# A two-layer hybrid decoder trunk on one core: projection blocks as one 512-column and one 256-column matmul, with an addition at eviction, and shorter softmaxes

## The chip, the cores and the metric

The kernel runs on one core of a Trainium2 chip. The metric is the device time of one execution in microseconds (us), the median of several runs. TensorE is PE in the rows (PEld is its weight loads), VectorE is DVE, ScalarE is ACT, GpSimd is POOL, and SyncE (SP) issues the weight transfers.

## What is computed

Two layers work on 256 tokens of width 2048, in fp32. Each layer normalises x, projects it with one large input matrix, feeds three mixers (sparse attention, an S5 state space, pooling), gates each, concatenates, projects with w_out, normalises and adds to x. Cut to what the change touches:

```python
def masked_softmax(s, mask, axis):
    s = jnp.where(mask, s.astype(jnp.float32), NEG_INF)
    m = jnp.max(s, axis=axis, keepdims=True)
    e = jnp.where(mask, jnp.exp(s - m), 0.0)
    return e / jnp.maximum(jnp.sum(e, axis=axis, keepdims=True), 1e-30)
...
p_c = masked_softmax(s_c, mask_c, -1)
...
p = masked_softmax(sc, mask, (-2, -1))
...
p_w = masked_softmax(s_w, mask_w, -1)
...
o = gates[..., 0, :] * o_c + gates[..., 1, :] * o_s + gates[..., 2, :] * o_w
```

With 256 tokens every causal block is among the selected ones, so the selected and the window branch are both plain causal attention, over different keys and values.

## The kernel before

**Two-part numbers.** Each fp32 operand of a large product is split into a high and a low part of a format that TensorE multiplies in one pass; the product is high times high, high times low and low times high, summed in PSUM. ACT makes the high part of each weight half piece (L311, 128x1024), DVE the low part (L317, the difference). The activations stand transposed in two tiles, hT[0] (high) and hT[1] (low), 16 blocks of 128 rows by 256 tokens.

**Pieces.** The weights of a layer come as a stream of pieces in the order of use, in halves of 512 KB. They land in a ring of five buffers (raw, RAWB = 5), and are split into a ring of four high (whi) and four low (wlo) buffers. Most pieces are 128 output columns of the input matrix: u5 (4 pieces), kc, vc, ks, kw (2 each), q, za (8 each), z5, up, zp (4 each), 40 in a layer and 80 in all. Function do_b handles such a piece: it splits the next piece's halves (split(n + 1, h)), multiplies the present one (mm_b, 16 blocks), and evicts it with what the piece asks for. For each block mm_b calls mm3, three matmuls of 256 columns into one PSUM tile pp, of which there are three:

```python
T.matmul(out, lhsT=lh, rhs=rh, start=start, stop=False, **kw)
T.matmul(out, lhsT=lh, rhs=rl, start=False, stop=False, **kw)
T.matmul(out, lhsT=ll, rhs=rh, start=False, stop=stop, **kw)
```

They are lines 387, 388 and 389. Other pieces are ck and cv (weights of the key and value compression, used straight from the raw buffer, L1111), vs and vw (values, with the activations as the stationary side), gl (the S5 mixer's GLU) and wo (output projection, 512 columns at a time, also through mm3).

**Evictions.** u5: two ACT copies (L1044, L1045). kc and vc: two DVE additions (cmp_blocks, L642). ks and kw: rope, four DVE operations, then a split (L697 to L700). q: an ACT copy to qf (L1128) and rope. za, z5, zp: silu2, a Tanh on ACT (L881) and one DVE operation (L882). up: an ACT copy (L1181).

**Chains.** Attention, the S5 scan, compression and pooling are generators that advance a step at a time between half pieces (slot), by a credit of estimated TensorE time. Outside the start and the layer boundary the tile scheduler then orders each engine's queue. att_unit handles one head, one tile of queries and two branches: scores, mask added to the diagonal (L724), maximum (L725), times -scale (L726), two Exp with sums, floor at 1e-30 (L732), reciprocal, gate, two scalings, transposes. There are 32 of them. att_cmp is the same for the compressed branch, 8 in all.

Of the kernel before, what the change touches and what calls it, by code (L numbers as in the profile page):

```python
# [18 lines left out]
NKT = D // 128  # L19
# [10 lines left out]
# column offsets of the input projection  # L30
# [4 lines left out]
def piece_plan():  # L35
    """Weight pieces of one layer in the order of use: (kind, index, cols per half)."""
    b = [("vs", 0), ("vs", 1)] + [("u5", t) for t in range(4)]
    early = [("kc", 0), ("kc", 1), ("vc", 0), ("vc", 1), ("ks", 0), ("ks", 1), ("kw", 0), ("kw", 1),
             ("vw", 0), ("vw", 1), ("vw", 2)]
    cmp_ = [("ck", i) for i in range(4)] + [("cv", i) for i in range(4)]  # L40
    mid = []
    for i, e in enumerate(early):
        mid.append(e)
        if i >= 2:
            mid += cmp_[:2]
            del cmp_[:2]
# [30 lines left out]
# columns of the per-layer small parameters  # L77
# [7 lines left out]
# columns of the per-layer S5 matrices, pool and compression matrices  # L85
# [5 lines left out]
for _n, _w in (("ident", 128), ("mask", 128), ("cos", 256), ("sin", 256), ("cmask", 32), ("valid", 2),  # L91
               ("rowm", 2), ("i2", 32), ("ptab", 64), ("tm", 16), ("m01", 64), ("hpi", 1)):
    CN[_n] = (_o, _o + _w)
    _o += _w
# [3 lines left out]
def constants():  # L98
# [7 lines left out]
    put("mask", np.where(i[None, :] <= i[:, None], 0.0, -1e30).astype(np.float32))  # L106
# [31 lines left out]
def body(ctx, tc, a):  # L138
# [113 lines left out]
        # cos and sin of 4 theta b and 32 theta a, a and b in 0 .. 7  # L252
# [38 lines left out]
    def split(n, h, hold=False):  # L291
        if n >= len(stream):
            return
        l, k, i, off = stream[n]
        if k in ("ck", "cv"):
            return
        hc = halves(k, i)
        w = hc[h]
        raw = raws.pop((n, h))
        if k == "wo" and i in (12, 13):  # L300
            if i == 12 and h == 0:
                X["hTw"] = tuple(z.rearrange("p k s -> p (k s)") for z in new_hT())
# [37 lines left out]
    def grab(*tags):  # L340
        """wait until every one of the tags has a free buffer, then hold them"""
# [5 lines left out]
    def demand(*tags):  # L347
        """the same for the stream of pieces: run the chains until the buffers are free"""
# [26 lines left out]
    def split_f32r(hi, lo, src, scale=None, hi_eng=None):  # L375
        """hi + lo == src * scale, both float32r"""
# [7 lines left out]
    def mm3(out, l, r, start, stop, **kw):  # L384
        """three passes: hi*hi, hi*lo, lo*hi"""
# [6 lines left out]
    def rstd_of(parts_, first=None):  # L392
        """(sum of the four parts / D + EPS) ** -0.5; first: what rstd_first made of three of them"""
# [11 lines left out]
    def norm_scale(x, r, gpre, hbuf, c):  # L405
        """hbuf = x * r * gpre in quarter c of x and hbuf [128, D]"""
# [3 lines left out]
    def norm_high(t, hbuf, hT, c):  # L410
        """high part of quarter c of hbuf transposed; returns what makes the low part"""
# [12 lines left out]
    def vsel(n, t, c):  # L424
        """values of the selected branch, tile t, from quarter c of hT"""
# [5 lines left out]
    def norm_vsel(n, t, x, r, gpre, hbuf, hT, lag):  # L431
        """the norm of tile t and its values, quarter after quarter"""
# [12 lines left out]
    def new_hT():  # L445
        return tuple(big.tile([128, NKT, S], F32R, name=nm("hT"), tag=f"hT{i}", bufs=1) for i in range(2))

# [1 line left out]
    def s5_chain(l):  # L449
# [22 lines left out]
        def tables(hf):  # L472
            """cos and sin of 4 theta j, j = 8 a + b, for the state tiles 8 hf .. 8 hf + 7"""
# [29 lines left out]
        def spread(dst, x, y, op, k0):  # L503
            """x op y, group by group into the block diagonal of dst"""
# [43 lines left out]
        for t in range(4):  # L548
# [5 lines left out]
            # transposed input matrices and the lag kernels  # L554
# [81 lines left out]
    def cmp_blocks(which, g, p, l):  # L636
# [3 lines left out]
        pv = p[:, :256].rearrange("p (n j) -> p j n", j=16)  # L640
# [53 lines left out]
    def rope(p, dst_hi, dst_lo):  # L694
        r1 = st([128, 256], "r1", bufs=2)
        r2 = st([128, 256], "r2", bufs=2)
        V.tensor_tensor(r1, p[:, :256], C["cos"], op=ALU.mult)  # L697
        V.tensor_tensor(r2[0:64], p[64:128, :256], C["sin"][64:128], op=ALU.mult)
        V.tensor_tensor(r2[64:128], p[0:64, :256], C["sin"][0:64], op=ALU.mult)
# [4 lines left out]
    def att_unit(pr, j, t):  # L704
        """one head of the pair, one tile of queries: scores .. transposed weights"""
# [15 lines left out]
        sv = st([128, 5, 2], "sv", bufs=4)  # L721
        P = st([128, 2, nk], "P", bufs=2)
        diag = pv[:, :, nk - 128:nk]
        V.tensor_tensor(diag, diag, bc(C["mask"][:, None, :], [128, 2, 128]), op=ALU.add)  # L724
        V.tensor_reduce(sv[:, 0], pv, axis=AX.X, op=ALU.max)  # L725
        V.tensor_scalar(sv[:, 1], sv[:, 0], -SCALE, None, op0=ALU.mult)  # L726
        for b in range(2):
            A.activation(P[:, b], pv[:, b], AF.Exp, scale=SCALE, bias=sv[:, 1, b:b + 1],  # L728
                         accum_out=sv[:, 2, b:b + 1])
        give("sc")  # L730
        yield 0.1 + 0.001 * 2 * nk
        V.tensor_scalar(sv[:, 3], sv[:, 2], 1e-30, None, op0=ALU.max)  # L732
        V.reciprocal(sv[:, 3], sv[:, 3])
        V.tensor_mul(sv[:, 4], X["gates"][:, t, 3 * h + 1:3 * h + 3], sv[:, 3])
        for b in range(2):
            A.activation(P[:, b], P[:, b], AF.Copy, scale=sv[:, 4, b:b + 1])  # L736
# [17 lines left out]
    def att_cmp(pr):  # L754
# [22 lines left out]
        sv = st([128, 4, 2, 2], "scv", bufs=2)  # L777
# [7 lines left out]
        V.tensor_scalar(sv[:, 1], sv[:, 1], 1e-30, None, op0=ALU.max)  # L785
        gt = X["gates"][:, :, 6 * p0:6 * p0 + 6].rearrange("p t (j b) -> p t j b", j=2)[:, :, :, 0]
        V.reciprocal(sv[:, 1], sv[:, 1])
        V.tensor_tensor(sv[:, 2], gt, sv[:, 1], op=ALU.mult)
        V.tensor_tensor(sv[:, 3], sv[:, 2], bc(C["valid"][:, :, None], [128, 2, 2]), op=ALU.mult)
        V.tensor_tensor(sc, sc, bc(sv[:, 3, :, :, None], [128, 2, 2, 16]), op=ALU.mult)  # L790
# [88 lines left out]
    def silu2(dst, p):  # L879
        """dst = 2*silu(p)"""  # L880
        A.activation(dst, p, AF.Tanh, scale=0.5)  # L881
        V.scalar_tensor_tensor(dst, dst, 1.0, p, op0=ALU.add, op1=ALU.mult)  # L882

# [48 lines left out]
    # start  # L932
# [91 lines left out]
    while n < nst:  # L1024
# [5 lines left out]
        if kind == "u5":  # L1030
# [23 lines left out]
        elif kind in ("kc", "vc"):  # L1054
# [8 lines left out]
            def ev(p, i=i, w=w, l=l):  # L1063
                cmp_blocks(w, i, p, l)

            do_b(n, ev)
        elif kind in ("ks", "kw"):
# [3 lines left out]
            do_b(n, lambda p, i=i, b=b: rope(p, X["kr"][:, 0, i, b, :], X["kr"][:, 1, i, b, :]))  # L1071
# [8 lines left out]
        elif kind == "vw":  # L1080
# [5 lines left out]
            for h in range(2):  # L1086
# [4 lines left out]
                if k0 == 16:  # L1091
                    vr = X["vr"]
                    for t in range(2):
# [3 lines left out]
                        V.tensor_scalar(X["gates"][:, t], X["gates"][:, t], 0.5, 0.5, op0=ALU.mult, op1=ALU.add)  # L1097
                slot(nk * 6 * w / 2400 - 1.1 * hv[h] / 1024 + 0.6)
# [17 lines left out]
        elif kind in ("q", "za"):  # L1116
# [9 lines left out]
            def ev(p, j=j, pr=pr, kind=kind):  # L1126
                if kind == "q":
                    A.activation(pr["qf"][:, j, :], p[:, :256], AF.Copy)  # L1128
                    rope(p, pr["qr"][:, 0, j], pr["qr"][:, 1, j])
# [8 lines left out]
                else:  # L1138
                    silu2(pr["zt"][:, j, :], p[:, :256])
# [4 lines left out]
        elif kind == "z5":  # L1144
            if i == 0:
                X["z5"] = a8([128, 4, 256])
            do_b(n, lambda p, i=i: silu2(X["z5"][:, i, :], p[:, :256]))
# [28 lines left out]
        elif kind == "up":  # L1176
            def ev(p, i=i, l=l):
# [3 lines left out]
                A.activation(pu[:, 16:], p[:, :256], AF.Copy)  # L1181
# [3 lines left out]
        elif kind == "zp":  # L1185
            def ev(p, i=i):
                demand("zs")
                z = st([128, 2, 256], "zs", bufs=2)[:, 0]
                silu2(z, p[:, :256])
                X["zp", i] = z  # L1190
            do_b(n, ev)
        else:
# [32 lines left out]
            def update(t, r, sq=None):  # L1225
                """x += og * r, with the sums of squares or the store"""
# [162 lines left out]
```

## Time and profile before

| what | value |
|---|---|
| time, median of 3 runs | 893.35 us (893.23 to 893.95) |
| profiled execution | span 890.6 us from the first to the last instruction; the page has no other time of it |
| median less span | 2.7 us, outside the recorded instructions |
| PE busy | 857.6 us, 96% of the span |
| DVE busy | 645.3 us, 72% |
| ACT busy | 481.3 us, 54% |
| granted TensorE clock | mean 0.988; below full at the start, at the layer boundary and at the very end |
| memory | 159.37 MB read and 4.19 MB written, 184 GB/s over the span |

A matmul's busy time runs from its start to a modelled end and overlaps the next matmul's. What a matmul costs in a stream is therefore the distance from its start to the next one's start (below: its pitch), not the duration in its row. An engine's busy share is an average over stages: the start, two layers of about 415 us each and the boundary between them near 450 us.

### The profile page before, as it was taken

The page shows a single profiled execution, that of the slowest core. Times are in us where ns is not written, and L with a number is a line of the kernel's source. Part 1 is how long each engine was busy: PE and PEld are TensorE (multiplying, and loading weights), DVE is VectorE, ACT ScalarE, POOL GpSimd, SP SyncE. Part 2 cuts the span into 40 slices and gives each one's busy share as a digit, 9 for nine tenths or more (in the row PEclk, how much of TensorE's full clock was granted, in tenths as well). Part 3 has the DMA queues.
Part 4 walks back from the last instruction along what each step waited for, and adds up shares of the span by engine and source line. Part 5 has one row for each costly group of instructions (what it writes and reads, how often), then busy time and mean ns, then how long its engine had stood idle before and what let it go on. Part 6 is the DMA issues. An engine that isn't in the chain of part 4 may idle for free. (4 is left out here: it accounts for less than half of the span.)

```text
span 890.6 us, 17313 instructions
## 1 busy us (share of the span) xinstructions
PE 857.6 (96%) x6848; PEld 795.3 (89%) x6848; DVE 645.3 (72%) x1264; ACT 481.3 (54%) x933; POOL 51.8 (6%) x71
## 2 busy tenths in 40 slices
PE   4899999999999999999979999999999999999996
PEld 3898889999999999888869988999999999998884
DVE  6886779796987866556478556978968878665563
ACT  5454635676566754445445525475847767344440
POOL 3302000000000000000040300000000000000000
PEclk9899999999999999999989999999999999999998
DMA  7565766524344665456445558663534347455642
GB/s 288 179 188 185 268 235 225 172 104 162 121 165 143 227 241 194 172 201 224 182 165 199 183 197 312 211 213 99 173 123 155 140 144 295 154 177 189 197 146 95
DMA packets 46042, 165.75 MB, mean 186 GB/s; under 512 B 5508, under 2 KB 5764, under 8 KB 44808
## 3 DMA queue, kind: packets, MB, share of 16 engines
q1 hardware_dynamic: 43352, 154.15, 50.3%
q0 software_dynamic: 2608, 10.49, 3.3%
q8 instruction: 54, 0.88, 0.4%
q14 instruction: 28, 0.23, 0.1%
HBM read 159.37 MB, written 4.19 MB: 184 GB/s over the span
## 5 line engine op out<-in xcount | busy, mean ns | idle before, releaser
L311 ACT ACTIVATE whi<-raw 128x1024 fp32r<-128x1024 f32 (+2 forms) x238 | 248.4, 1046 | 256.3 <-PE pp L388 82.8
L317 DVE TENSOR_TENSOR wlo<-raw,whi 128x1024 fp32r<-128x1024 f32 (+1 forms) x236 | 284.4, 1207 | 123.7 <-ACT whi L311 123.1
L389 PE MATMUL pp<-hT,wlo 128*128 128x256 f32 x1280 | 365.7, 286 | 0.5 <-DVE wlo L317 0.5
L387 PE MATMUL pp<-hT,whi 128*128 128x256 f32 x1280 | 364.8, 285 | 0.8 <-ACT whi L311 0.8
L388 PE MATMUL pp<-hT,whi 128*128 128x256 f32 x1280 | 363.5, 284 | 0.0
L387 PEld LDWEIGHTS pp<-hT,whi 128*128 128x128 f32 x1280 | 245.0, 191 | 6.1 <-issue 3.8
L389 PEld LDWEIGHTS pp<-hT,wlo 128*128 128x128 f32 x1280 | 245.0, 191 | 2.4 <-DVE wlo L317 0.7
L388 PEld LDWEIGHTS pp<-hT,whi 128*128 128x128 f32 x1280 | 245.0, 191 | 1.7 <-issue 1.0
L387 PE MATMUL acc<-whi,m 128*128 128x512 f32 x112 | 44.4, 397 | 0.0
L389 PE MATMUL acc<-whi,m 128*128 128x512 f32 x112 | 44.4, 397 | 0.0
L388 PE MATMUL acc<-wlo,m 128*128 128x512 f32 x112 | 44.1, 394 | 0.0
L388 PE MATMUL pp<-wlo,m 128*128 128x512 f32 x112 | 43.6, 389 | 0.0
L389 PE MATMUL pp<-whi,m 128*128 128x512 f32 x112 | 43.6, 389 | 0.0
L387 PE MATMUL pp<-whi,m 128*128 128x512 f32 x112 | 43.6, 389 | 0.0
L507 ACT ACTIVATE m<-m 64x256 f32<-64x256 f32 x64 | 26.4, 413 | 5.9 <-DVE m L505 4.9
L728 ACT ACTIVATE P<-sc,sv 128x128 f32<-128x128 f32 (+1 forms) x64 | 26.2, 418 | 5.4 <-DVE sv L726 3.7
L925 POOL DMA_DIRECT2D a<-in_gpost x2 | 1.1, 557 | 451.4 <-PE tr L743 451.4
L378 ACT ACTIVATE a<-tr 128x256 fp32r<-128x256 f32 (+1 forms) x32 | 15.6, 488 | 18.6 <-PE tr L743 18.5
L387 PEld LDWEIGHTS acc<-whi,m 128*128 128x128 f32 x112 | 21.5, 192 | 4.5
L388 PEld LDWEIGHTS acc<-wlo,m 128*128 128x128 f32 x112 | 21.5, 192 | 4.5
L389 PEld LDWEIGHTS acc<-whi,m 128*128 128x128 f32 x112 | 21.4, 191 | 4.5
L736 ACT ACTIVATE P<-P,sv 128x128 f32<-128x128 f32 (+1 forms) x64 | 25.4, 448 | 0.0
(295 smaller groups left out, 1384.4 us busy)
## 6 DMA issues: line engine op xcount, KB each, us to landing
raw<-in_w SPq DMA_DIRECT2D x272, 512.0 KB, 3.6
raw<-in_w SPq DMA_DIRECT2D x8, 420.0 KB, 4.2
a<-in_x SPq DMA_DIRECT2D x4, 512.0 KB, 6.9
a<-in_gpost POOLq DMA_DIRECT2D x2, 1024.0 KB, 4.8
a<-in_x POOLq DMA_DIRECT2D x2, 1024.0 KB, 6.3
xs<-a SPq DMA_DIRECT2D x2, 1024.0 KB, 4.1
a<-xs POOLq DMA_DIRECT2D x2, 1024.0 KB, 7.4
out_dram<-a SPq DMA_DIRECT2D x8, 256.0 KB, 2.4
```

The costliest lines, as they stand in the source:

```text
L311: A.activation(hi[:, :w], raw[:, :w], AF.Copy)
L317: V.tensor_tensor(lo[:, :w], raw[:, :w], hi[:, :w].bitcast(F32), op=ALU.subtract)
L378: A.activation(hi, src, AF.Copy)
L387: T.matmul(out, lhsT=lh, rhs=rh, start=start, stop=False, **kw)
L388: T.matmul(out, lhsT=lh, rhs=rl, start=False, stop=False, **kw)
L389: T.matmul(out, lhsT=ll, rhs=rh, start=False, stop=stop, **kw)
L507: A.activation(dst[64 * g:64 * g + 64, :, k0:k0 + 4, 16 * g:16 * g + 16], x[64 * g:64 * g + 64], AF.Copy)
L728: A.activation(P[:, b], pv[:, b], AF.Exp, scale=SCALE, bias=sv[:, 1, b:b + 1], accum_out=sv[:, 2, b:b + 1])
L736: A.activation(P[:, b], P[:, b], AF.Copy, scale=sv[:, 4, b:b + 1])
L925: nc.gpsimd.dma_start(g, bass.AP(tensor=src.tensor, offset=src.offset, ap=[[0, 128], [1, D]]))
```

## The change

The two activation tiles become one tile, so that the high and the low half of a block can be read as one operand of 512 columns. mm2 takes the place of mm3 in mm_b: the high weights times both halves in one matmul over all 512 columns of pp, then the low weights times the high half into the first 256. join adds the two halves of pp: an ACT copy of columns 256 to 511 into a small buffer (r2, of which there are two), then a DVE addition. Every one of the 80 pieces is evicted through join, and rope, cmp_blocks and silu2 then read its sum from SBUF. In att_unit two tensor_tensor_reduce, one for each branch, add the mask (now 256 columns wide), scale by the negative scale and take the minimum; the floor is gone. In att_cmp the floor and the multiplication by the valid mask are gone, and the gates are multiplied by it once a layer (gcmp). RAWB is 5 in both kernels.

```diff
-for _n, _w in (("ident", 128), ("mask", 128), ("cos", 256), ("sin", 256), ("cmask", 32), ("valid", 2),
+for _n, _w in (("ident", 128), ("mask", 256), ("cos", 256), ("sin", 256), ("cmask", 32), ("valid", 2),
...
+    def mm2(p, l, r, start, stop):
+
+        T.matmul(p.rearrange("p (z s) -> p z s", z=2), lhsT=l[0], rhs=r, start=start, stop=False)
+        T.matmul(p[:, :256], lhsT=l[1], rhs=r[:, 0], start=False, stop=stop)
+
+    def join(p, y):
+
+        z = st([128, 256], "r2", bufs=2)
+        A.activation(z, p[:, 256:], AF.Copy)
+        V.tensor_tensor(y, p[:, :256], z, op=ALU.add)
+        return y
...
     def new_hT():
-        return tuple(big.tile([128, NKT, S], F32R, name=nm("hT"), tag=f"hT{i}", bufs=1) for i in range(2))
+        z = big.tile([128, 2, NKT, S], F32R, name=nm("hT"), tag="hT", bufs=1)
+        return z[:, 0], z[:, 1], z
...
-        diag = pv[:, :, nk - 128:nk]
-        V.tensor_tensor(diag, diag, bc(C["mask"][:, None, :], [128, 2, 128]), op=ALU.add)
-        V.tensor_reduce(sv[:, 0], pv, axis=AX.X, op=ALU.max)
-        V.tensor_scalar(sv[:, 1], sv[:, 0], -SCALE, None, op0=ALU.mult)
+
         for b in range(2):
-            A.activation(P[:, b], pv[:, b], AF.Exp, scale=SCALE, bias=sv[:, 1, b:b + 1],
-                         accum_out=sv[:, 2, b:b + 1])
+            V.tensor_tensor_reduce(out=pv[:, b], in0=pv[:, b], in1=C["mask"][:, 256 - nk:], scale=-SCALE,
+                                   scalar=3.0e38, op0=ALU.add, op1=ALU.min, accum_out=sv[:, 0, b:b + 1])
+        for b in range(2):
+            A.activation(P[:, b], pv[:, b], AF.Exp, scale=-1.0, bias=sv[:, 0, b:b + 1],
+                         accum_out=sv[:, 1, b:b + 1])
         give("sc")
         yield 0.1 + 0.001 * 2 * nk
-        V.tensor_scalar(sv[:, 3], sv[:, 2], 1e-30, None, op0=ALU.max)
...
     def silu2(dst, p):
...
-        A.activation(dst, p, AF.Tanh, scale=0.5)
-        V.scalar_tensor_tensor(dst, dst, 1.0, p, op0=ALU.add, op1=ALU.mult)
...
+        join(p, dst)
+        t = st([128, 256], "r1", bufs=2)
+        A.activation(t, dst, AF.Tanh, scale=0.5)
+        V.scalar_tensor_tensor(dst, t, 1.0, dst, op0=ALU.add, op1=ALU.mult)
...
-            mm3(p[:, :256], (hi[:, sl], lo[:, sl]), (hT[0][:, k, :], hT[1][:, k, :]), k == 0, k == 15)
+            mm2(p, (hi[:, sl], lo[:, sl]), hT[2][:, :, k, :], k == 0, k == 15)
...
             def ev(p, i=i):
-                A.activation(X["uT"][:, i, :], p[:, :256], AF.Copy)
-                A.activation(X["utb"][:, i], p[:, :256].rearrange("p (j b) -> p b j", b=4), AF.Copy)
+                u = join(p, X["uT"][:, i, :])
+                A.activation(X["utb"][:, i], u.rearrange("p (j b) -> p b j", b=4), AF.Copy)
...
-                cmp_blocks(w, i, p, l)
+                cmp_blocks(w, i, join(p, st([128, 256], "qf")), l)
...
-                    A.activation(pr["qf"][:, j, :], p[:, :256], AF.Copy)
-                    rope(p, pr["qr"][:, 0, j], pr["qr"][:, 1, j])
+                    rope(join(p, pr["qf"][:, j, :]), pr["qr"][:, 0, j], pr["qr"][:, 1, j])
```

**PE, first layer, where the first vc piece ends and the ck pieces begin.** Of a block the last matmuls are shown (pp is the piece's PSUM tile, whi and wlo the split weights, acc<-raw the ck matmuls, tr and sc steps of the S5 chain). Before:

```order
L387 MATMUL pp_890<-hT_84,whi_840 128x256
L388 MATMUL pp_890<-hT_85,whi_840 128x256
L389 MATMUL pp_890<-hT_84,wlo_841 128x256
L563 MATMUL tr_946<-cn,m_66_461 128x128 x4
L1111 MATMUL acc_955<-raw_720,a_94_724 32x256 x4
L1111 MATMUL acc_955<-raw_722,a_94_724 32x256 x4
L1111 MATMUL acc_955<-raw_801,a_94_724 32x256 x3
L587 MATMUL sc_966<-a_60_428,m_68_463 128x64 x4
```

With the change:

```order
L394 MATMUL pp_809<-hT_84,whi_763 128x512
L395 MATMUL pp_809<-hT_84,wlo_764 128x256
L577 MATMUL tr_790<-cn,m_65_452 128x128
L394 MATMUL pp_917<-hT_84,whi_891 128x512
L1128 MATMUL acc_862<-raw_663,a_97_667 32x256
L577 MATMUL tr_790<-cn,m_65_452 128x128 x3
L1128 MATMUL acc_862<-raw_663,a_97_667 32x256 x3
L1128 MATMUL acc_862<-raw_665,a_97_667 32x256 x4
L1128 MATMUL acc_862<-raw_732,a_97_667 32x256 x4
```

A block is two matmuls instead of three, the first with twice the columns, and the first block of the next vc piece (pp_917) now stands ahead of the ck matmuls.

**ACT, the same place.** L311 and L312 are the high splits of the weights (whi), L400 is the copy of join, and the m tiles belong to the S5 chain. Before:

```order
L311 ACTIVATE whi_840<-raw_638 128x1024
L507 ACTIVATE m_66_461<-m_68_463 64x16x16 x2
L507 ACTIVATE m_66_461<-m_67_462 64x16x16 x2
L311 ACTIVATE whi_984<-raw_884 128x1024
L507 ACTIVATE m_67_462<-m_68_463 64x4x4x16 x2
L507 ACTIVATE m_67_462<-m_67_462 64x4x4x16 x2
L572 ACTIVATE m_68_463<-tr_871 128x512
L534 ACTIVATE m_67_462<-a_60_428 64x4x16 x2
```

With the change:

```order
L312 ACTIVATE whi_763<-raw_595 128x1024
L400 ACTIVATE r_106_718<-pp_671 128x256
L400 ACTIVATE r_115_784<-pp_736 128x256
L312 ACTIVATE whi_891<-raw_803 128x1024
L521 ACTIVATE m_65_452<-m_67_454 64x16x16 x2
L521 ACTIVATE m_65_452<-m_66_453 64x16x16 x2
L521 ACTIVATE m_66_453<-m_67_454 64x4x4x16 x2
L400 ACTIVATE r_123_848<-pp_809 128x256
L521 ACTIVATE m_66_453<-m_66_453 64x4x4x16 x2
L586 ACTIVATE m_67_454<-tr_790 128x512
L312 ACTIVATE whi_901<-raw_805 128x1024
```

The copies of join for the pieces kc (pp_671, pp_736) and vc (pp_809), which had no operation on ACT, now stand between the weight splits, ahead of the splits for the next vc piece (whi_891, whi_901). The orders of SP and of POOL are the same in both.

## Rows read from the trace of the kernel before

**Rows 1.** The page's first part: busy time, share of the span, instructions of each engine.
```profile
PE 857.6 (96%) x6848; PEld 795.3 (89%) x6848; DVE 645.3 (72%) x1264; ACT 481.3 (54%) x933; POOL 51.8 (6%) x71
```
**Rows 2.** Waits of PE: engine, line, releaser, us in total, times, longest.
```profile
PE pp L387 <- ACT whi L311: 0.8, 1, 0.8
PE pp L389 <- DVE wlo L317: 0.5, 1, 0.5
```
**Rows 3.** Timeline of PE in a q piece: start us, modelled us, line, operands.
```profile
250.07 0.28 PE L387 MATMUL pp<-hT,whi 128*128 128x256 f32 x1
...
250.43 0.28 PE L387 MATMUL pp<-hT,whi 128*128 128x256 f32 x1
```
**Rows 4.** Timeline of PE in the output projection, the same columns.
```profile
400.12 0.39 PE L387 MATMUL acc<-whi,m 128*128 128x512 f32 x1
...
400.80 0.39 PE L387 MATMUL acc<-whi,m 128*128 128x512 f32 x1
```
**Rows 5.** Timeline of PE, score matmuls between blocks of a piece, the same columns.
```profile
181.27 0.28 PE L388 MATMUL pp<-hT,whi 128*128 128x256 f32 x1
181.39 0.40 PE L387 MATMUL sc<-a,qr 128*128 128x512 f32 x1
181.63 0.40 PE L388 MATMUL sc<-a,qr 128*128 128x512 f32 x1
181.86 0.39 PE L389 MATMUL sc<-a,qr 128*128 128x512 f32 x1
182.09 0.28 PE L389 MATMUL pp<-hT,wlo 128*128 128x256 f32 x1
182.21 0.28 PE L387 MATMUL pp<-hT,whi 128*128 128x256 f32 x1
```
**Rows 6.** Costliest groups: line, operands, count, then busy us, mean ns, idle before.
```profile
L389 PE MATMUL pp<-hT,wlo 128*128 128x256 f32 x1280 | 365.7, 286 | 0.5 <-DVE wlo L317 0.5
```
**Rows 7.** Stretches: length, busy us (count) by engine, clock, DMA share, GB/s.
```profile
95.00:131.00 36.00, 35.35 (x384) 30.91 (x377) 24.45 (x48) 20.07 (x38) 0.00 (x0) 1.00 0.80 284
131.00:165.00 34.00, 34.00 (x341) 32.95 (x340) 30.94 (x59) 21.19 (x42) 0.00 (x0) 1.00 0.62 206
165.00:320.00 155.00, 155.00 (x1378) 149.73 (x1377) 127.94 (x307) 103.32 (x235) 1.64 (x3) 1.00 0.45 159
531.00:566.00 35.00, 33.83 (x324) 30.65 (x317) 27.49 (x57) 18.63 (x36) 0.00 (x0) 1.00 0.79 283
```
**Rows 8.** Waits between 88 and 131 us, and between 531 and 566 us.
```profile
ACT whi L311 <- DMA raw<-in_w: 19.5, 6, 8.8
...
ACT whi L311 <- DMA raw<-in_w: 10.2, 6, 3.4
```
**Rows 9.** Groups of PE between 95 and 131 us, and between 531 and 566 us.
```profile
L387 PE MATMUL pp<-hT,whi 128*128 128x256 f32 x62 | 17.8, 288 | 0.0
...
L387 PE MATMUL pp<-hT,whi 128*128 128x256 f32 x64 | 18.6, 290 | 0.8 <-ACT whi L311 0.8
```
**Rows 10.** Groups of ACT over the whole span, shapes apart.
```profile
L311 ACT ACTIVATE whi<-raw 128x1024 fp32r<-128x1024 f32 x226 | 238.5, 1058 | 243.3 <-PE pp L388 73.8 <-PE acc L389 51.2 <-issue 50.8
L1128 ACT ACTIVATE qf<-pp 128x256 f32<-128x256 f32 x16 | 5.9, 370 | 0.0
```
**Rows 11.** Groups of DVE over the whole span, shapes apart.
```profile
L724 DVE TENSOR_TENSOR sc<-sc,cn 128x256 f32<-128x256 f32 x32 | 13.6, 425 | 6.4 <-PE sc L389 6.4
L725 DVE TENSOR_REDUCE sv<-sc 128x2 f32<-128x512 f32 x16 | 11.0, 685 | 0.1
L700 DVE TENSOR_TENSOR r<-r,r 128x256 f32<-128x256 f32 x24 | 10.1, 421 | 0.3
L725 DVE TENSOR_REDUCE sv<-sc 128x2 f32<-128x256 f32 x16 | 6.7, 418 | 0.0
L726 DVE TENSOR_SCALAR sv<-sv 128x2 f32<-128x2 f32 x32 | 5.0, 158 | 0.1
L977 DVE DVE_READ_ACCUMULATOR a<-a 128x1 f32 x1 | 0.1, 81 | 0.0
```

More of the change, by code (lines that the diff above doesn't have):

```diff
@@ L105, in constants @@
     i = np.arange(128)
-    put("mask", np.where(i[None, :] <= i[:, None], 0.0, -1e30).astype(np.float32))
+    tri = np.where(i[None, :] <= i[:, None], 0.0, -1e30).astype(np.float32)
+    put("mask", np.concatenate([np.zeros((128, 128), np.float32), tri], axis=1))
     half = 64
@@ L301, in split @@
             if i == 12 and h == 0:
-                X["hTw"] = tuple(z.rearrange("p k s -> p (k s)") for z in new_hT())
+                X["hTw"] = tuple(z.rearrange("p k s -> p (k s)") for z in new_hT()[:2])
             o = ((i - 12) * 2 + h) * 1024
@@ L639, in cmp_blocks @@
         bf = X["blkf" + which]
-        pv = p[:, :256].rearrange("p (n j) -> p j n", j=16)
+        pv = p.rearrange("p (n j) -> p j n", j=16)
         for h in range(2):
@@ L696, in rope @@
         r2 = st([128, 256], "r2", bufs=2)
-        V.tensor_tensor(r1, p[:, :256], C["cos"], op=ALU.mult)
-        V.tensor_tensor(r2[0:64], p[64:128, :256], C["sin"][64:128], op=ALU.mult)
-        V.tensor_tensor(r2[64:128], p[0:64, :256], C["sin"][0:64], op=ALU.mult)
+        V.tensor_tensor(r1, p, C["cos"], op=ALU.mult)
+        V.tensor_tensor(r2[0:64], p[64:128], C["sin"][64:128], op=ALU.mult)
+        V.tensor_tensor(r2[64:128], p[0:64], C["sin"][0:64], op=ALU.mult)
         V.tensor_tensor(r1, r1, r2, op=ALU.add)
@@ L720, in att_unit @@
         yield from grab("P")
-        sv = st([128, 5, 2], "sv", bufs=4)
+        sv = st([128, 3, 2], "sv", bufs=4)
         P = st([128, 2, nk], "P", bufs=2)
-        diag = pv[:, :, nk - 128:nk]
-        V.tensor_tensor(diag, diag, bc(C["mask"][:, None, :], [128, 2, 128]), op=ALU.add)
-        V.tensor_reduce(sv[:, 0], pv, axis=AX.X, op=ALU.max)
-        V.tensor_scalar(sv[:, 1], sv[:, 0], -SCALE, None, op0=ALU.mult)
         for b in range(2):
-            A.activation(P[:, b], pv[:, b], AF.Exp, scale=SCALE, bias=sv[:, 1, b:b + 1],
-                         accum_out=sv[:, 2, b:b + 1])
+            V.tensor_tensor_reduce(out=pv[:, b], in0=pv[:, b], in1=C["mask"][:, 256 - nk:], scale=-SCALE,
[3 more added lines that the diff above has]
+                         accum_out=sv[:, 1, b:b + 1])
         give("sc")
         yield 0.1 + 0.001 * 2 * nk
-        V.tensor_scalar(sv[:, 3], sv[:, 2], 1e-30, None, op0=ALU.max)
-        V.reciprocal(sv[:, 3], sv[:, 3])
-        V.tensor_mul(sv[:, 4], X["gates"][:, t, 3 * h + 1:3 * h + 3], sv[:, 3])
+        V.reciprocal(sv[:, 1], sv[:, 1])
+        V.tensor_mul(sv[:, 2], X["gates"][:, t, 3 * h + 1:3 * h + 3], sv[:, 1])
         for b in range(2):
-            A.activation(P[:, b], P[:, b], AF.Copy, scale=sv[:, 4, b:b + 1])
+            A.activation(P[:, b], P[:, b], AF.Copy, scale=sv[:, 2, b:b + 1])
         yield 0.4
@@ L776, in att_cmp @@
         sc = st([128, 2, 2, 16], "scs", bufs=2)
-        sv = st([128, 4, 2, 2], "scv", bufs=2)
+        sv = st([128, 3, 2, 2], "scv", bufs=2)
         V.tensor_tensor(sc, pv, bc(cmask[:, :, None, :], [128, 2, 2, 16]), op=ALU.add)
@@ L784, in att_cmp @@
         V.tensor_reduce(sv[:, 1], sc, axis=AX.X, op=ALU.add)
-        V.tensor_scalar(sv[:, 1], sv[:, 1], 1e-30, None, op0=ALU.max)
-        gt = X["gates"][:, :, 6 * p0:6 * p0 + 6].rearrange("p t (j b) -> p t j b", j=2)[:, :, :, 0]
+        gt = X["gcmp"][:, :, 6 * p0:6 * p0 + 6].rearrange("p t (j b) -> p t j b", j=2)[:, :, :, 0]
         V.reciprocal(sv[:, 1], sv[:, 1])
         V.tensor_tensor(sv[:, 2], gt, sv[:, 1], op=ALU.mult)
-        V.tensor_tensor(sv[:, 3], sv[:, 2], bc(C["valid"][:, :, None], [128, 2, 2]), op=ALU.mult)
-        V.tensor_tensor(sc, sc, bc(sv[:, 3, :, :, None], [128, 2, 2, 16]), op=ALU.mult)
+        V.tensor_tensor(sc, sc, bc(sv[:, 2, :, :, None], [128, 2, 2, 16]), op=ALU.mult)
         yield 0.5
@@ L1070, in body @@
             b = 0 if kind == "ks" else 1
-            do_b(n, lambda p, i=i, b=b: rope(p, X["kr"][:, 0, i, b, :], X["kr"][:, 1, i, b, :]))
+            do_b(n, lambda p, i=i, b=b: rope(join(p, st([128, 256], "qf")), X["kr"][:, 0, i, b, :], X["kr"][:, 1, i, b, :]))
         elif kind == "vs":
@@ L1097, in body @@
                         V.tensor_scalar(X["gates"][:, t], X["gates"][:, t], 0.5, 0.5, op0=ALU.mult, op1=ALU.add)
+                    X["gcmp"] = st([128, 2, 24], "gcmp")
+                    V.tensor_tensor(X["gcmp"], X["gates"], bc(C["valid"][:, :, None], [128, 2, 24]), op=ALU.mult)
                 slot(nk * 6 * w / 2400 - 1.1 * hv[h] / 1024 + 0.6)
@@ L1138, in ev @@
                 else:
-                    silu2(pr["zt"][:, j, :], p[:, :256])
+                    silu2(pr["zt"][:, j, :], p)
                     if j == 1:
@@ L1146, in body @@
                 X["z5"] = a8([128, 4, 256])
-            do_b(n, lambda p, i=i: silu2(X["z5"][:, i, :], p[:, :256]))
+            do_b(n, lambda p, i=i: silu2(X["z5"][:, i, :], p))
         elif kind == "gl":
@@ L1180, in ev @@
                 V.memset(pu[:, :16], 0.0)
-                A.activation(pu[:, 16:], p[:, :256], AF.Copy)
+                join(p, pu[:, 16:])
                 X["pu", i] = pu
@@ L1188, in ev @@
                 z = st([128, 2, 256], "zs", bufs=2)[:, 0]
-                silu2(z, p[:, :256])
+                silu2(z, p)
                 X["zp", i] = z
```

## The prediction

> **What bounds the kernel now.** I read the page's busy times first. PE is busy for 857.6 of 890.6 us, DVE for 645.3, ACT for 481.3 [rows 1]. A modelled busy time proves little, so the list of what PE waited for came next. In the weight pieces it is almost empty: 0.8 us in all for a high split and 0.5 us for a low one [rows 2]. ACT, which makes the high splits, is the one that waits: most of the 243.3 us of idle time ahead of its 226 full splits ended when PE freed a weight buffer [rows 10]. The splits run as early as the ring of four lets them, and PE sets the pace.
>
> Then I read the pitch of the matmuls in the timeline. In a piece's block of three 256-column matmuls, from one L387 to the next takes 0.36 us, so each costs 0.120 [rows 3]. In the output projection three 512-column matmuls take 0.68 us, so each costs 0.227 [rows 4]. Twice the columns cost 0.227 instead of 0.240: some 13 ns of each matmul do not depend on its columns. The granted clock is full in all of this [rows 7], the 2.4 GHz level.
>
> Last, the stretches. From 95 to 131 us and from 531 to 566 us, where ck and cv pass through the ring, PE is not quite full (35.35 of 36, 33.83 of 35) and the transfers run at 284 and 283 GB/s, against 159 from 165 to 320 us [rows 7]. There ACT waits for weights, 19.5 and 10.2 us [rows 8]. These two stretches follow the weight stream, and a faster PE gains nothing in them.
>
> **The change, part by part.** *Matmuls.* 80 pieces of 16 blocks are 1280 blocks; the group of L389 has just that count [rows 6]. A block was three pitches of 0.120, 0.360 us. It becomes one of 512 columns and one of 256. The 512 columns are two runs of 256, in two halves of one tile, which no row shows for this operand. The nearest are the plain 512 columns at 0.227 [rows 4] and the score matmuls at 0.24, 0.23 and 0.23, the only ones that stand between 256-column blocks of the same pieces [rows 5]. Two of the score matmuls are followed by another of 512, mean 0.235, and the third by one of 256. I take 0.227, since all three are back-to-back matmuls of 512 columns, it is the mean of three pitches in steady state, and nothing in the score rows is named as the cause of their surplus. The 256 columns cost 0.12 before and after the score matmuls too [rows 5]. A block then takes 0.347, 13.3 ns less; with 0.235 it takes 0.355, 5 ns less. Over 1280 blocks that is **17.1 us** (end: 6.4). The timeline prints steps of 10 ns, so a mean over three pitches is known to some 3 ns, 4.3 us over 1280; the other end is 21.4.
>
> *What the weight stream keeps.* In the two stretches 62 and 64 blocks run [rows 9]. At 13.3 ns each, 126 blocks would give 1.7 us, which I count as lost. Left: **15.4 us** (ends 5.8 for the score pitch, 21.4 for the best pitch with nothing lost).
>
> *Joins on DVE.* 80 additions of 128x256 at 0.42, the price of rope's addition [rows 11]: 33.6 us. They lie beside PE.
>
> *Softmax on DVE.* Of 32 units the mask addition (13.6), both maxima (11.0 and 6.7) and the scaling (5.0) go [rows 11], 36.3 us, and a floor that is as small as the scaling besides. Two fused operations come for each unit. Not in the trace; I bound them below by nothing and above by a 256-wide addition and its accumulator read, 0.42 + 0.08 [rows 11], for both widths: 64 x 0.50 = 32 us. I take 32. At least 4 us are saved, and DVE gains some 29 us in all, 645 to 674 of then 875, 77%. Nothing on the path that sets the end, as long as PE's splits keep their lead. Where that is thin, from 131 to 165 us, DVE is busy for 30.94 of 34 [rows 7], and four joins of ks and kw (1.7 us in a layer) fall on it or just ahead; 3.1 us are free there. I take nothing, and keep 3.4 us for both layers as an end.
>
> *Joins on ACT.* u5, q and up trade one copy for another. The other 48 pieces get a copy more, 0.37 each [rows 10]: 17.8 us, on an engine at 54%. It waits for the piece's last matmul. Behind it in ACT's queue stand the next weight splits, and PE waits for these a piece or more later; the lead that ACT shows [rows 10] covers it. In PSUM a piece is held until the DVE addition, and three pp buffers rotate, one piece each 5.5 us (16 x 0.347). rope held its tile through three DVE operations before.
>
> *What costs nothing.* The one tile for both activation halves is written and freed where the two were: only at the start and at the boundary. The mask makes one early transfer of constants longer by 64 KB, some 0.2 us at 284 GB/s. SP and POOL keep their orders. The small buffers r1, r2 and qf, which the joins now share, are read by DVE within a few operations; a wait there holds ACT, under the same lead.
>
> **The sum.** 15.4 us off the profiled execution's 890.6 makes a span of 875.2. The median of the runs, 893.35, stands 2.7 above that span, and nothing outside it changes: **878.0 us**.
>
> **Rivals.** *A, the wide matmul hardly pays.* If the operand in two runs costs 0.235, as the score matmuls do, 1154 blocks outside the two stretches give 5 ns each, 5.8 us: **887.6 us**. For it speaks that these are the only wide matmuls between such blocks; against it, that the plain ones show 0.227. The Trainium skill has a rule that points the same way: by TensorE: Matmul & The Clock Gate, section Back-to-back issue gap, a warm matmul costs its columns at 2.4 GHz plus some 2.5 ns, so that dropping 1280 matmuls would be an estimated 3.2 us, for 890.2. The trace disagrees: two pitches of 256 exceed one of 512 by 13 ns [rows 3, 4], not by 2.5.
>
> *B, slower: the joins hold up the weight splits.* The copy of join for kc and vc stands ahead of the next splits on ACT, for pieces that had nothing on ACT before. It can't run until its piece is done, where a split could run once the buffer's half piece is; that holds a split by up to half a piece, 8 x 0.360 = 2.9 us. In the two stretches the lead is gone already (PE's longest wait for a split, 0.8 us, lies there [rows 2, 9]). About 8 pieces run in them (126 blocks). If all 8 holds come through to PE, 23.2 us are lost against 15.4 won: **901.2 us**. It decides from the sixth uncovered hold on. For it: the order of ACT, as shown. Against: the stretches are paced by transfers, and a split that is held while its weights are still on the way loses nothing.
>
> *C, the same with few holds, or DVE short of time between 131 and 165 us.* Two to five holds (5.8 to 14.5 us) leave **883.8 to 892.5 us**.
>
> *D, the change does not do what it says,* for instance a 512-column operand in two runs being executed as two matmuls: no gain, and the additions hidden: **893.4 us**.
>
> **Chances.** The forecast (871 to 884) has 0.68, A 0.11, C 0.12, B 0.06, D 0.03. The range from 871 to 889 takes in the forecast, A and about half of C, some 0.85. It reaches below the best end of the sum (872.0) by 1 us, since a DVE that is freed in the softmaxes may let a late step come sooner. A measurement of this kernel tells 0.2%, 1.8 us, from no change. Faster by more than that: forecast, A and most of C, 0.88. Within: the rest of C and D, 0.05. Slower: B and a little of C, 0.07.
>
> **What would show it.** In the changed kernel a block's two matmuls should start 0.347 us apart from the next block's, the wide one at 0.227 (A: 0.235 or more). PE's list of waits should stay under some 3 us in the pieces; tens of us for whi or wlo would be B or C, and would lie between 95 and 165 us and between 531 and 600. DVE should be busy for 660 to 680 us and ACT for about 499. The fused softmax operation should read 0.5 us or less with its accumulator read. The output projection keeps 0.227. I am wrong in the mechanism if the pitch falls as said and the time doesn't, or if the time falls by more than 22 us.

## The result, and the profile after

The changed kernel takes **905.24 us** (median of 4 runs, 904.63 to 908.23) against 893.29 of the kernel before beside it: a ratio of 1.0151, 95% interval 1.0135 to 1.0168. It is 12 us slower by these medians and 13.5 by the ratio, where the prediction said 15.4 faster (878.0). The profiled execution is the longest of the four: 908.23 us, with a span of 906.4.

In the changed kernel mm3 is lines 388 to 390, the wide matmul is L394 and the narrow one behind it L395; join copies in L400 (ACT) and adds in L401 (DVE); the fused softmax operation is L739. The page's busy times, which answer to [rows 1]:

```profile
PE 858.7 (95%) x5568; PEld 729.8 (81%) x5568; DVE 662.4 (73%) x1330; ACT 501.1 (55%) x981; POOL 51.7 (6%) x71
```

DVE and ACT are what was forecast. PE has 1280 matmuls fewer and is busy for as long as before. Two of a block's matmuls in the timeline of PE answer to [rows 3] (columns: start, modelled us, engine, line, operands):

```profile
196.07 0.40 PE L394 MATMUL pp<-hT,whi 128*128 128x512 f32 x1
196.31 0.28 PE L395 MATMUL pp<-hT,wlo 128*128 128x256 f32 x1
196.43 0.40 PE L394 MATMUL pp<-hT,whi 128*128 128x512 f32 x1
```

From block to block it is 0.36 here; the median over all 1280 starts is 0.350, against 0.360 before. So the block did become shorter, by 10 ns. The list of PE's waits answers to [rows 2] (waited for, releaser, us in all, times, longest):

```profile
PE pp L388 <- DVE mr L1188: 7.0, 2, 3.5
...
PE pp L394 <- DVE a L401: 2.5, 2, 1.3
PE pp L394 <- DVE qf L401: 2.2, 2, 1.2
PE pp L394 <- ACT whi L312: 1.5, 1, 1.5
PE tr L807 <- DVE a L380: 1.5, 2, 0.7
```

The weight splits (whi) are 1.5 us of it. The rest is new: PE waits for PSUM tiles that DVE has not evicted, twice for the GLU (L1188, once in each layer), four times for a join (L401). The stretches, as in [rows 7]:

```profile
95.00:131.00 36.00, 36.00 (x310) 26.72 (x307) 30.41 (x60) 21.24 (x41) 0.00 (x0) 1.00 0.82 284
131.00:165.00 34.00, 34.00 (x292) 30.49 (x290) 32.14 (x64) 19.96 (x38) 0.00 (x0) 1.00 0.64 198
165.00:320.00 155.00, 147.90 (x1019) 127.68 (x1020) 121.01 (x303) 101.19 (x236) 1.10 (x2) 0.97 0.50 146
300.00:330.00 30.00, 25.75 (x161) 23.64 (x161) 20.69 (x53) 19.43 (x46) 1.63 (x3) 0.89 0.60 204
531.00:566.00 35.00, 32.23 (x315) 24.03 (x314) 23.81 (x49) 16.41 (x34) 0.00 (x0) 0.95 0.78 263
```

From 165 to 320 us PE was full before; now 7.1 us are missing. DVE is not fuller there than it was (121.01 busy, 127.94 before), so DVE's total work is not the reason. The order of its queue can be: at 198.49 us PE waits for a join that stands in DVE's queue behind steps of the S5 chain (L543, L551 and L519), which run back to back (in brackets: idle just before, and what ended it):

```profile
198.49 0.50 PE L394 MATMUL pp<-hT,whi 128*128 128x512 f32 x1 [1.20 <-DVE qf L401]
...
197.01 0.42 DVE L543 TENSOR_TENSOR m<-a,akt 128x256 f32<-128x256 f32 x1
197.35 0.42 DVE L551 TENSOR_TENSOR m<-a,akt 128x256 f32<-128x256 f32 x1
197.68 0.42 DVE L519 TENSOR_TENSOR m<-m 128x256 f32<-128x256 f32 x1
198.02 0.42 DVE L401 TENSOR_TENSOR qf<-pp,r 128x256 f32<-128x256 f32 x1
```

The largest hole within a layer, in the timeline of PE and then of DVE:

```profile
309.95 0.28 PE L390 MATMUL pp<-m,wlo 128*128 128x256 f32 x1
310.97 0.38 PE L807 MATMUL tr<-cn,scs 128*32 128x128 f32 x2 [0.74 <-DVE a L380]
314.86 0.58 PE L388 MATMUL pp<-m,whi 128*128 128x256 f32 x1 [3.50 <-DVE mr L1188]
315.23 0.41 PE L389 MATMUL pp<-m,whi 128*128 128x256 f32 x1
315.45 0.41 PE L390 MATMUL pp<-m,wlo 128*128 128x256 f32 x1
...
319.50 0.35 PE L388 MATMUL pp<-m,whi 128*128 128x256 f32 x1
319.68 0.28 PE L389 MATMUL pp<-m,whi 128*128 128x256 f32 x1
```

```profile
306.74 0.42 DVE L1186 SCALAR_TENSOR_TENSOR r<-r,a 128x256 f32<-128x256 f32 x1
309.46 0.69 DVE L847 TENSOR_TENSOR mr<-acc,zs 128x512 f32<-128x512 f32 x1 [2.30 <-PE acc L390]
...
311.95 1.23 DVE L318 TENSOR_TENSOR wlo<-raw,whi 128x1024 fp32r<-128x1024 f32 x1 [0.51 <-ACT whi L312]
313.09 0.68 DVE L383 SCALAR_TENSOR_TENSOR m<-mr,m 128x512 fp32r<-128x512 f32 x1
313.81 0.47 DVE L813 SCALAR_TENSOR_TENSOR pct<-tr,cn,pct 32x256 fp32r<-32x256 f32 x1
314.32 0.48 DVE L1188 SCALAR_TENSOR_TENSOR mr<-pp,sm,r 128x256 f32<-128x256 f32 x1
```

The last GLU half piece wants a pp tile that an earlier half still holds. Its eviction (L1188) writes mr, of which there is one buffer; the attention output of the pair before (L847) has it and gives it back at L383. That output is late because its matmuls on acc stand amid the GLU in PE's queue, and no block of another piece stands there for PE to do meanwhile. None of these instructions is a join. Behind the hole 256 columns take 0.21 us instead of 0.12, and the granted clock of the stretch is 0.89: a part of it ran at the 1.2 GHz level, behind 4.8 us in which PE did no more than two transposes. The Trainium skill, in TensorE: Matmul & The Clock Gate, Part 1: The HAM clock gate, says that the clock follows how busy the engine was of late; this row agrees.

### The profile page after: what moved, and what is told of

It reads as the page before. It is cut to its first block, busy times and chain, and to the rows that moved or that the text cites. A ratio compares the mean times of both kernels' runs of the same rounds, so it can differ in the third digit from the quotient of the medians.

```text
span 906.4 us, 14884 instructions
## 1 busy us (share of the span) xinstructions
PE 858.7 (95%) x5568; PEld 729.8 (81%) x5568; DVE 662.4 (73%) x1330; ACT 501.1 (55%) x981; POOL 51.7 (6%) x71
## 5 line engine op out<-in xcount | busy, mean ns | idle before, releaser
L394 PE MATMUL pp<-hT,whi 128*128 128x512 f32 x1280 | 463.0, 402 | 6.3 <-DVE a L401 2.5
L312 ACT ACTIVATE whi<-raw 128x1024 fp32r<-128x1024 f32 (+2 forms) x238 | 248.9, 1048 | 229.8 <-PE pp L394 101.2
L395 PE MATMUL pp<-hT,wlo 128*128 128x256 f32 x1280 | 363.7, 284 | 0.5 <-DVE wlo L318 0.5
L394 PEld LDWEIGHTS pp<-hT,whi 128*128 128x128 f32 x1280 | 241.8, 189 | 67.5 <-issue 4.9
L395 PEld LDWEIGHTS pp<-hT,wlo 128*128 128x128 f32 x1280 | 243.2, 190 | 5.2 <-DVE wlo L318 1.9
L400 ACT ACTIVATE r<-pp 128x256 f32<-128x256 f32 x80 | 29.7, 372 | 5.9 <-PE pp L395 5.6
L388 PE MATMUL pp<-m,whi 128*128 128x256 f32 x64 | 20.3, 317 | 7.0 <-DVE mr L1188 7.0
```

Of the source, the lines that this page charges most:

```text
L394: T.matmul(p.rearrange("p (z s) -> p z s", z=2), lhsT=l[0], rhs=r, start=start, stop=False)
L395: T.matmul(p[:, :256], lhsT=l[1], rhs=r[:, 0], start=False, stop=stop)
L400: A.activation(z, p[:, 256:], AF.Copy)
```

## The experiments

Theory J: the joins cost the time. Theory S: the softmaxes do. Theory O: the tile scheduler orders the queues anew for the changed instructions, and the new order has holes.

**e1, e2, e3, e4: the parts apart.**

e1 takes the changed kernel and puts mm3 and the evictions of the kernel before back (first edit below); e2 puts the softmaxes of before back; e3 the evictions of before alone, from p[:, :256]; e4 has the second edit, in mm2.

```diff
-            mm2(p, (hi[:, sl], lo[:, sl]), hT[2][:, :, k, :], k == 0, k == 15)
+            mm3(p[:, :256], (hi[:, sl], lo[:, sl]), (hT[0][:, k, :], hT[1][:, k, :]), k == 0, k == 15)
...
-        T.matmul(p.rearrange("p (z s) -> p z s", z=2), lhsT=l[0], rhs=r, start=start, stop=False)
+        if start:
+            T.matmul(p.rearrange("p (z s) -> p z s", z=2), lhsT=l[0], rhs=r, start=True, stop=False)
+        else:
+            T.matmul(p[:, :256], lhsT=l[0], rhs=r[:, 0], start=False, stop=False)
+            T.matmul(p[:, 256:], lhsT=l[0], rhs=r[:, 1], start=False, stop=False)
```

> Only the leaner softmaxes: the pieces keep three matmuls of 256 columns and the evictions of the kernel before. Theory J (the joins at eviction cost the time: a PSUM tile of a piece is freed only when the DVE addition has had its turn in a DVE queue that is full around 185 and 630 us): nothing is joined here and DVE has 16 us less to do than in the changed kernel, so PE stays as full as before and the time is 890 to 894 us. Theory S (the softmax change itself costs the time, by the order of its operations): about 905 us. Theory O (the tile scheduler makes another order out of any change, and a new order leaves holes in PE): anywhere from 890 to 905 us, with holes of PE at other places than in the changed kernel.

> Only the wide matmul with its joins: the softmaxes are those of the kernel before. Theory J: DVE has some 20 us more to do than in the changed kernel, the full stretches are longer, and the time is 906 to 915 us. Theory S: without the fused softmax the gain of the shorter blocks comes through, 880 us. Theory O: anywhere from 880 to 915 us.

> The wide matmul and the leaner softmaxes, but nothing is joined: the evictions are those of the kernel before and read the first 256 columns alone, so the product of the weights' high part with the activations' low part is left out of the pieces. Theory J: the gain of the block (0.350 us by the changed kernel's trace against 0.360, 1280 times, 12.8 us) comes through: 878 to 883 us. Theory O: the pieces are as short as in the changed kernel, the chains meet PE at the same unfavourable places, and the time stays above 890 us. Theory S: about 905 us.

> The joins and the leaner softmaxes without the wide matmul: in 15 of 16 blocks of a piece the weight-high part is multiplied with the two activation halves in two matmuls of 256 columns into the two halves of the PSUM tile (the first block of a piece stays wide). The blocks take 0.36 us as before, the joins are all there. Theory J: the joins cost what they cost in the changed kernel (905.2 less 880.5, some 25 us) or somewhat less because pieces come at the old rate: 905 to 918 us. Theory O: no holes where the old rate is kept: 890 to 897 us.

Measured: e1 892.77 us, ratio 1.0008 (0.9997 to 1.0019). e2 916.23, 1.0272 (1.0257 to 1.0287). e3 895.24, 1.0032 (1.0013 to 1.0051). e4 898.31, 1.0070 (1.0055 to 1.0085). S falls with e1. e2 lies above every range that was set, and e4 between O's and J's. As the whole cause J falls with e3: without a single join the wide matmul still gains nothing. But e3 is 10.6 us under the change, so the joins are not cleared yet. The holes of e3 are at the GLU again, and its blocks are as short as the change's. O is left, with some cost of the joins.

**e5, e6, e7, e8: the order held by hand.** A table of numbers, taken from the built program of one kernel, ties each instruction of a queue behind the one that stood ahead of it there. The instructions stay the same.

```diff
+def impose(tc):
...
+        row = [ins[i + s] for i, s in enumerate(shift)]
+        for x, y in zip(row, row[1:]):
...
+            tc.add_manual_dep(y, x.name, mybir.DependencyInfo(mybir.DependencyClass.NoSync,
+                                                              mybir.DependencyReason.DATA), reason="order")
             body(ctx, tc, aps)
+            impose(tc)
```

> The changed kernel, instruction for instruction, but each engine's queue is held in the order that the tile scheduler made for the kernel with joins and three narrow matmuls (e4), with the wide matmul where the first of its two narrow ones stood. Theory O (the time went into the new order of the queues, not into the joins or the block): e4 ran 898.3 us, the block is 10 ns shorter 1200 times, 12 us: 886 us, within 884 to 889. Theory B (with shorter pieces the DVE queue, which is full around 185, 235, 630 and 670 us, or the weights set the pace whatever the order): 896 to 905 us.

> The kernel with the wide matmul and no joins (e3, which leaves the product with the activations' low part out of the pieces), each queue held in the order of the kernel with the leaner softmaxes alone (e1). Theory O: e1 ran 892.8 us, 1280 blocks are 10 ns shorter, 12.8 us: 880 us, within 878 to 883. Theory B: no better than e3 itself, 893 to 895 us.

> The reverse: the kernel with joins and narrow matmuls (e4, 898.3 us in its own order), each queue held in the order of the changed kernel, the second narrow matmul right behind the first. Theory O: the holes of the changed kernel open here too and the blocks are 10 ns longer: 910 to 918 us. Theory B: pieces at the old rate leave DVE and the weights enough time in any order: 898 to 903 us.

> The changed kernel with TensorE's queue alone in the order of e4; the scheduler still orders VectorE, ScalarE and the DMA queues. If it is TensorE's order that costs the time: 886 to 890 us, as in the kernel with all queues held. If it is the order on VectorE and ScalarE (what stands ahead of a step that PE waits for): 898 to 906 us.

Measured: e5 885.91 us, ratio 0.9933 (0.9918 to 0.9948). e6 877.93, 0.9846 (0.9832 to 0.9861). e7 914.17, 1.0250 (1.0233 to 1.0267). e8 885.38, 0.9929 (0.9909 to 0.9949). e5 and e7 lie in O's ranges and e6 0.1 us under its range, so B falls; e8 lies 0.6 us under the range for TensorE's order and far from the other. The same instructions are 2.2% faster in e4's order than in the scheduler's own, and the narrow kernel, 0.7% slower than before in its own order, is 2.5% slower in the changed kernel's; so a table as such brings no gain. The change with a table of its own order was not run. Of e7 the hole at the GLU is the same to the digit:

```profile
312.64 0.38 PE L811 MATMUL tr<-cn,scs 128*32 128x128 f32 x2 [0.74 <-DVE a L380]
316.52 0.58 PE L388 MATMUL pp<-m,whi 128*128 128x256 f32 x1 [3.50 <-DVE mr L1192]
```

In e8 PE's queue alone is held in e4's order, and nothing is lost against e5: holding PE is enough. That does not say which queue's order costs the time. By line and tile, in the order of their starts in the traces, 624 of the 1330 DVE instructions of e8 stand at another place than in the change, and 169 at another place than in e5. With PE held, the scheduler puts most of DVE's queue into e4's order too.

**e10, e11, e12, e13: which part of the order, and what the joins cost in a good one.**

e10 has this edit and no table:

```diff
-            slot(1.41)
+            slot(1.76)
...
-        slot(1.6)
+        slot(2.0)
```

e11, e12 and e13 hold PE's queue by a table as above. In e11 the table is the change's own order with the places 1426 to 1940 and 3904 to 4418 of 4964 taken from e4's, in e12 with the places 905 to 1400 and 3383 to 3876, and in e13 the whole is e1's.

> The changed kernel with the chains advanced more eagerly between half pieces (credits of 1.76 and 2.0 where 1.41 and 1.6 stood), no queue held by hand. In the order of the changed kernel the transposes of the attention weights (L757) stand on average 10 blocks of a piece later than in e4's order; with these credits 2. If the lateness of the chains in TensorE's order is what costs the time: 886 to 896 us. If only the exact places count: 900 to 910 us.

> The changed kernel with TensorE's queue held: its own order everywhere but in the late stretch of each layer (from the pieces at 250 us to those at 339, and at 692 to 780), where it is e4's. The joined kernel fell behind by some 7 us there in each layer while its pieces should have gained 1. Theory P (the cost arises place by place): 905 less 12 to 15, 890 to 893 us. Theory Q (a chain that is late since 190 us stays late): 898 to 905 us.

> The same for the early stretch of the attention alone: e4's order from 167 to 246 us and from 612 to 687 us, the changed kernel's own elsewhere. There it fell behind by some 5 us in the first layer and 3 in the second. Theory P: 895 to 899 us. Theory Q: this stretch carries the rest, 886 to 892 us.

> The changed kernel with TensorE's queue in the order of e1 (leaner softmaxes alone, three narrow matmuls, no joins); the other queues are left to the scheduler. It differs from e6 (877.9 us) by the joins alone, as far as TensorE's order goes. If the joins cost little by themselves once the order is right: 878 to 882 us. If the joins cost what e5 and e6 differ by: 885 to 887 us.

Measured: e10 923.31 us, ratio 1.0364 (1.0330 to 1.0398): both readings missed. The chains stand earlier, and now PE meets them before DVE and ACT are ready (timeline of PE in e10):

```profile
199.42 0.38 PE L757 MATMUL tr<-cn,P 128*128 128x128 f32 x2
201.84 0.74 PE L582 MATMUL sc<-m,m 128*32 128x128 f32 x16 [2.04 <-ACT P L742]
202.52 0.69 PE L757 MATMUL tr<-cn,P 128*128 128x128 f32 x2
...
205.32 0.90 PE L757 MATMUL tr<-cn,P 128*128 128x128 f32 x3 [2.11 <-DVE a L380]
```

So lateness is not the cause as such. These rows and those at the GLU suggest that what counts is whether a block of a piece stands beside each chain step; no run varied that alone. e11 took 896.85, 1.0062 (1.0044 to 1.0079), between P's range and Q's; e12 901.57, 1.0117 (1.0084 to 1.0151), a little over P's and far from Q's. Against the change's 1.0151 that is 7.9 and 3.0 us of the 19.4 by which e5 beats it, and the 3.0 are not clear of nothing, since e12's interval reaches up to 1.0151. The early stretch does not carry the rest, so Q falls in its strong form, and some 8 us lie outside both or arise only from the two together (not separated; between 74 and 131 and between 531 and 566 us the orders differ too).

e13 took 883.84, 0.9921 (0.9892 to 0.9951), between its two readings. PE is full again, in one row from 165 to 320 us, and at the GLU no gap is left behind the transposes:

```profile
165.00:320.00 155.00, 155.00 (x1092) 135.05 (x1091) 130.26 (x321) 108.21 (x249) 1.64 (x3) 1.00 0.52 164
```

```profile
296.23 0.28 PE L390 MATMUL pp<-m,wlo 128*128 128x256 f32 x1
296.35 0.38 PE L807 MATMUL tr<-cn,scs 128*32 128x128 f32 x2
296.49 0.36 PE L388 MATMUL pp<-m,whi 128*128 128x256 f32 x1
```

It does 1092 matmuls in the 155 us where the change did 1019, with DVE busier (130.26). But it stands 0.0075, 6.7 us, behind e6. Its PE waits for steps of the S5 chain (L629, L577) and of the compression (L668) where e6's did not:

```profile
PE acc L629 <- DVE m L623: 2.1, 1, 2.1
PE sc L668 <- ACT P L662: 0.9, 1, 0.9
PE tr L577 <- ACT m L521: 0.7, 1, 0.7
```

**e14, e15: the pitch, and the joins.** Twelve runs left two terms open.

```diff
-        z = big.tile([128, 2, NKT, S], F32R, name=nm("hT"), tag="hT", bufs=1)
-        return z[:, 0], z[:, 1], z
+        z = big.tile([128, NKT, 2, S], F32R, name=nm("hT"), tag="hT", bufs=1)
+        return z[:, :, 0], z[:, :, 1], z
...
+            if stream[n][1] in ("u5", "kc", "vc"):
+                mm3(p[:, :256], (hi[:, sl], lo[:, sl]), (hT[0][:, k, :], hT[1][:, k, :]), k == 0, k == 15)
```

The first edit is e14's, the second e15's, whose evictions of these pieces are those of the kernel before.

> The kernel of e13 (the change, TensorE's queue in e1's order, 883.8 us) with the high and the low half of each activation block side by side, so that the wide matmul reads one run of 512 columns instead of two of 256. If the two runs cost the 6 ns by which the wide matmul (0.233 us) exceeds the one of the output projection (0.227): the pitch falls to 0.227, 1280 times 6 ns are 7.7 us, and the time is 876 to 879 us. If the surplus comes from standing between narrow matmuls: the pitch stays 0.233 and the time 883 to 885 us.

> The kernel of e13 with the three narrow matmuls and the evictions of the kernel before in the pieces u5, kc and vc (16 of 80), the ones beside which the S5 steps run that PE waited for at 74 to 99 and at 523 us in e13. 256 blocks gain 10 ns less, 2.6 us. If the joins of these pieces are what cost e13 its 6 us against e6: 6 saved and 2.6 lost, 880 to 881 us. If the joins cost time everywhere a little: 885 to 886 us.

Measured: e14 884.66 us, ratio 0.9917 (0.9894 to 0.9941), as e13. The pitch is what it was (timeline of PE in e14, wide matmul L395):

```profile
250.05 0.39 PE L395 MATMUL pp<-hT,whi 128*128 128x512 f32 x1
250.28 0.28 PE L396 MATMUL pp<-hT,wlo 128*128 128x256 f32 x1
250.40 0.39 PE L395 MATMUL pp<-hT,whi 128*128 128x512 f32 x1
250.63 0.28 PE L396 MATMUL pp<-hT,wlo 128*128 128x256 f32 x1
```

The median from a wide start to the narrow one is 0.232 (0.233 in the change), from the narrow to the wide 0.117; the output projection keeps 0.227 in both. The two runs cost nothing, then. What the surplus of 6 ns is due to stays open. It stands where wide and narrow take turns, but taking turns can't be all of it: in the kernel before, 26 of the 32 score matmuls of 512 columns with another such behind them took 0.235 or 0.236 as well, as in [rows 5]. e15 took 882.24, 0.9893 (0.9867 to 0.9918), between its two readings and within e13's interval. By the ratios it is 2.5 us better, with 256 blocks fewer that gain (2.6 us), so the 16 joins beside the S5 steps would be some 5 of the 6.7 us. That is a lean and not shown.

e15 has the lowest median of the complete kernels here, 1.1% under the kernel before; it needs its table.

## Why the prediction was wrong

The step that failed is the one under *Matmuls* that takes what a block saves for what the kernel saves: "PE sets the pace", so the gain comes through outside the two stretches of the weight stream. That held PE's order to be the same. The prediction spoke of the order of ACT, SP and POOL and not of PE's, though the section on the kernel says that the tile scheduler orders each queue, and the section on the change shows PE's order altered at one place. No rival was a new order on PE. What the runs showed in its place: the new order cost some 20 us, more than the 14.5 us that the shorter blocks bring when the order is held. The mark that the text set itself came in: the pitch fell and the time didn't.

Step by step, in ratios against the kernel before times 892 us:

| step | runs compared | us | forecast |
|---|---|---|---|
| softmaxes | e1 | +0.7 (not distinguishable from 0) | 0 |
| wide matmul, order held | e6 against e1 | -14.5 | -15.4 |
| joins, PE's order held | e13 against e6 | +6.7 | 0 |
| the scheduler's order | the change against e13 | +20.5 | none |
| all | the change | +13.5 | -15.4 |

The steps come from runs at different times: by the medians, each against its own kernel before, the order is 18.4 us instead of 20.5. In e6 all queues are held and in e13 PE's alone, so the 6.7 us hold whatever the scheduler's order of the other queues costs.

- *The block.* 0.347 forecast, 0.350 measured (median); 1280 times 10 ns are 12.8 us instead of 17.1, within the ends given. The 0.227 of the output projection was the wrong neighbour by 6 ns (the score matmuls' 0.235 was off by 2), and the narrow matmul gave 3 ns back (0.117 for 0.120). e6 came to 14.5 all the same: its pieces' matmuls, start to start, sum to 459.7 us against 472.0 in e1, 12.3; where the other 2.2 come from was not traced.
- *Rival A* (0.235) was right on the wide matmul alone and wrong on the block. By the rule it cited from the Trainium skill (TensorE: Matmul & The Clock Gate, Back-to-back issue gap) a block would be 2.5 ns shorter; the trace shows 10. The section gives that formula for an isolated matmul, and says that in a stream the weight loads set the spacing too, so the rule was not meant for these blocks.
- *Joins.* Their duration was right (L401 0.418 and L400 0.372 in the rows below), and so was what they replace. "The lead that ACT shows [rows 10] covers it" looked at the wrong thing: with whi the lead held, since PE waited 1.5 us for it in all. The term that was put at nothing measured 6.7 us in a good order. Of the 5.3 us by which the profiled spans of e13 and e6 differ (881.3 and 876.0), 3.7 are the waits shown above; how the joins delay these steps was not traced.
- *Rival B* forecast 901.2, near the truth, but by held weight splits, of which PE's 1.5 us for whi (0.8 before) show next to nothing. Its nearness is luck.
- *The fused softmax.* 32 us were taken for 64 of them; the rows below say 13.6 + 9.3 + 8.7 = 31.6. 0.56 at 256 columns with its accumulator read is a little over the 0.5 that was set, 0.43 at 128 under it. DVE fell by 11.8 us in e1 (633.5), which bought nothing.
- *Two readings.* [rows 7] have no stretch around 400 us, where the output projection's pitch was read; the trace shows the clock full from 395 to 440 us. The 2.7 us between the median and the span are not all outside the recorded instructions: the later runs have some 1.8 there (908.23 and 906.4 here), so the profiled execution was shorter than the median. Neither moves the forecast.

The groups of the changed kernel by shape (busy us, mean ns, idle before):

```profile
L401 DVE TENSOR_TENSOR qf<-pp,r 128x256 f32<-128x256 f32 x40 | 16.7, 418 | 1.4 <-ACT r L400 1.3
L739 DVE CUSTOM_DVE_ANT_0 sc<-sc,cn 128x256 f32<-128x256 f32 x32 | 13.6, 424 | 0.1
L739 DVE CUSTOM_DVE_ANT_0 sc<-sc,cn 128x128 f32<-128x128 f32 x32 | 9.3, 290 | 0.1
L739 DVE DVE_READ_ACCUMULATOR2_ANT sv<- 128x1 f32 x64 | 8.7, 137 | 0.1
```

```profile
L400 ACT ACTIVATE r<-pp 128x256 f32<-128x256 f32 x80 | 29.7, 372 | 5.9 <-PE pp L395 5.6
```

**Left open.** Why the scheduler places the chains elsewhere once the matmul is wide was not looked into; that the wide matmul alone does it is shown by e3 against e6 (17 us apart, the same instructions). Which queue's order costs the time was not separated. The change in the kernel before's own PE order was not tried, and neither were buffers of their own for the joins, which share r1 and r2 with the S5 chain.

## What to carry to other kernels

Where a scheduler orders the queues, the time of a change is the time of its instructions in an order that you have not seen: compare the built order on the bounding engine first, and price the places where PE has no independent block beside a chain step. To tell a bad instruction from a bad order, hold the order and swap the instructions, and the reverse; four runs showed here that the order costs the time, where PE's list of waits names DVE. A busy share of 95% with 1280 matmuls fewer is a warning: modelled busy time hides short holes and a lower clock.

## What the hardware showed that was not expected

A matmul's start-to-start time is not its columns and a constant. 512 columns took 0.227 us in the output projection, 0.233 in the block ahead of 256 and 0.235 or 0.236 among most of the score matmuls of the kernel before; 256 took 0.120 in the old block and 0.117 ahead of the wide matmul in the new one. Whether the operand lies in one run or two makes no difference (e14); what makes it was not found. And a hole costs more than its length: behind the 3.8 us at 311 us, PE's 256 columns came every 0.21 us until 319.5, some 20 matmuls with 0.09 us more each, 1.8 us on top.
